# A mixer's output projection by Strassen's seven products instead of eight block products, with its transposes and loads placed anew

## The chip, the cores and the metric

The kernel runs on one core of a Trainium2 chip. The metric is the device time of one execution in microseconds; the time of a kernel is the median over its runs. Engines are called PE (TensorE), DVE (VectorE), ACT (ScalarE), POOL (GpSimd) and SP (SyncE). Each engine works through its own instructions in one fixed order; SP, ACT and POOL also start DMA transfers, each on a queue of its own.

## The reference

One decoder layer on 512 tokens of width 1024, in float32. The part around the change:

```python
y_a = pool_mixer(z_pool, w_pool[i], pool_scale[i]) @ w_branch_a[i]
y_b = spatial_gating(z_uv, sgu_norm[i], w_spatial[i], b_spatial[i]) @ w_branch_b[i]
x = x + (g_a * y_a + g_b * y_b) @ w_out[i]      # the output projection
h = rmsnorm(x, ffn_norm[i])                     # a convolutional FFN and an embedding gate follow
```

`w_out` is 1024 x 1024, as are `w_branch_a` and `w_branch_b`.

## The kernel before

**Numbers in two parts.** Every float32 operand of a matmul is split into a rounded part and a remainder (`hi`, `lo`); `mm3` makes a product of three matmuls (hi·hi, hi·lo, lo·hi). For a weight, `parts` writes `whi` on ACT and `wlo` on DVE; for activations, `split` and `cut_into` do the same (`blk`, `cmb`, `a11`).

**Weights.** A weight arrives in chunks of 512 KB in a buffer `raw`, by SP's queue. `todo` lists all chunks in the order of their use; `prepare` starts up to four loads ahead and `take` keeps up to three chunks split and ready. `whi` and `wlo` have four buffers each, `raw` shares 37 blocks of 4 KB a partition (`blk`) with most activations. The tile framework sets semaphores and decides the order on each engine; a buffer is handed on when its last reader is done.

**Two ways to multiply.** `by_token` does one half of the output columns (`fh`) at a time: four PSUM banks, one for each block of 128 tokens, eight row blocks `k`, 24 matmuls of 512 columns for a chunk. `seven` does a product of 2 x 2 blocks by Strassen's scheme in Winograd's form: seven products `P1` to `P7`, each of half the rows, half the tokens and half the columns, that is 12 matmuls for a chunk of two row blocks (`pairs_of`). `combine` makes the four sums of activation blocks (`D`, `S2`, `S3`, `E`), and `plan_seven` the sums of weight blocks, in one of several ways: with `adds="vector"` DVE adds them, with `"some"` part of them, with `"all"` none: then a DMA of POOL's queue adds a block from memory onto the `raw` buffer (`add_to`). `"P6"`, `"P7"` and `"P4"` accumulate onto two banks `sd` (`seeded`) into which ACT has copied the result of `P1`, and ACT copies them out after `P6` and after `P7` (`copies`).

**The stage in question.** The branch product `yp @ w_branch_a` runs by `by_token` (lines 571 to 576); DVE multiplies it with the gate and adds the other branch into `ga`. `later` is a tiny DVE copy that makes a following DMA wait: the loads of the residual `x` (4 x 512 KB, `xr`) and of the embedding input `pt` (2 x 256 KB, `pT`) go out on ACT's queue. PE transposes `ga` (32 transposes, `turned`), `split` cuts them into `m`, and the output projection runs by `by_token` (lines 622 to 627): 8 chunks, 192 matmuls. Its results are added to `x`. The embedding product (24 matmuls, `embed`), a norm and 32 more transposes follow, then the FFN, whose down projection uses `seven` in the order `DOWN` with `"some"`.

Of the kernel before, what the change touches and what calls it, by code (L numbers as in the profile page):

```python
# [44 lines left out]
def trunk(ctx, tc, xT, xr, pT, wsT, par, bsp, w_u0, w_u1, w_v, w_ga, w_gb, w_p, w_pl,  # L45
# [38 lines left out]
    def pairs_of(n):  # L84

        return [(q, min(2, n - q)) for q in range(0, n, 2)]

    def plan(src, cols=CW, **kw):
        got = []
        todo.append((lambda: got.append(load_raw(src)), lambda: parts(got[0], cols, **kw)))  # L90

    def plan_seven(w, order=INNER, adds="vector", spare=(), q0=0, n=HK):

# [50 lines left out]

        return [unit(prod, ch) for prod in order for ch in pairs_of(n)]

# [33 lines left out]
    for i in range(KD):  # L180
        plan(w_a[i // 4, i % 4].rearrange(flat))
    for i in range(KD):
        plan(w_o[i // 4, i % 4].rearrange(flat))
    for k in range(2):
# [25 lines left out]
    def act(b, sl=slice(None)):  # L210
        return b[:, 0, sl], b[:, 1, sl]
# [30 lines left out]
    def later(t, src):  # L242

        V.tensor_copy(t, src)
# [101 lines left out]

    def seven(op, drain, order=INNER, fill=()):


        fill = list(fill)  # L350
        n = len(op)
        bank_of = {}
# [19 lines left out]

        for prod in order:
            b, c = ops[prod]
            if b not in bank_of:
                bank_of[b] = seeded if b == "b" else [bank() for _ in range(2)]
            o = bank_of[b]
            first = b != "b" and b not in begun
            begun.add(b)
            for ch in pairs_of(n):  # L380
                step(o, c, take(), ch, first)
                if fill:
                    fill.pop(0)()
            if prod == "P1":
                for j in range(2):
                    S.copy(seeded[j], o[j])
            elif prod == "P6":
                copies(0)
            elif prod == "P7":
                copies(1)  # L390
                minus(1)
                for j in range(2):
                    drain(1, j, 1, u[1][j])
            elif prod == "P4":
                for j in range(2):
                    drain(1, j, 0, seeded[j])
            elif prod == "P2":
                for j in range(2):
                    drain(0, j, 0, o[j])
            elif prod == "P3":  # L400
                minus(0)
                for j in range(2):
                    drain(0, j, 1, u[0][j])
# [5 lines left out]

    def by_token(acts, fh, banks, kps, between=None):  # L410

        for kp in kps:
            c = take()
            for b in range(NT):
                for kk in range(2):
                    k = 2 * kp + kk
                    mm3(banks[b], act(acts[k], slice(b * P, (b + 1) * P)), wslice(c, kk, T), k == 0, k == KD - 1)


# [149 lines left out]


    for fh in range(2):
        banks = [bank() for _ in range(NT)] if fh == 0 else [bank(), *seeded, bank()]
        by_token(yp, fh, banks, range(KD // 2))
        for b in range(NT):
            V.tensor_tensor(ga[b][:, fh], banks[b], ga[b][:, fh], op=ALU.mult)
            V.tensor_tensor(ga[b][:, fh], ga[b][:, fh], gb[b][:, fh], op=ALU.add)

    x = [block("x") for _ in range(NT)]
    for b in range(NT):
        later(x[b][:, 0, :1], ga[0][:, 0, :1])  # L580
        nc.scalar.dma_start(x[b].rearrange("p a t -> p (a t)"), xr[b])

    pp = []
    for k in range(2):
        pt = work("pt")
        later(pt[:, :1], ga[0][:, 0, :1])
        nc.scalar.dma_start(pt, pT[k])
        pp.append(act(split(pt)))
# [16 lines left out]

    def columns(z, b, f):

        return z[b][:, f // HK, f % HK * P:(f % HK + 1) * P]

    def turned(z, f):  # L610

        tp = bank()
        for b in range(NT):
            PE.transpose(tp[:, b * P:(b + 1) * P], columns(z, b, f), ident)  # L614
        return tp


    m = []
    for f in range(KD):
        m.append(split(turned(ga, f)))  # L620
    xss = [small.tile([P, 2], F32, tag="xss", name="xss", bufs=NT) for _ in range(NT)]
    for fh in range(2):
        banks = [bank() for _ in range(NT)] if fh == 0 else [*seeded, bank(), bank()]
        by_token(m, fh, banks, range(KD // 2))
        for b in range(NT):
            V.tensor_tensor(x[b][:, fh], banks[b], x[b][:, fh], op=ALU.add)
            squares(b, fh, xss)

# [164 lines left out]
def _layout(i):  # L793
# [9 lines left out]
    def th(w):  # L803
        return w.reshape(KD // 2, 2, P, 2, T).transpose(3, 0, 2, 1, 4)

    def sv(w):
        return w.reshape(2, HK, P, 2, T).transpose(0, 3, 1, 2, 4).reshape(4, HK, P, T)
# [8 lines left out]
    def pairs(z):  # L816
# [21 lines left out]
        "w_b": th(a["w_branch_b"][0]),  # L838
        "w_o": th(a["w_out"][0]),
        "w_up": pairs(up),  # L840

        "w_dn": a["w_down"][0].reshape(KF // 2, 2, P, 2, T).transpose(1, 3, 0, 2, 4).reshape(4, KF // 2, P, T),
        "w_g": a["w_ple_gate"][0].reshape(KD, P, D),
# [18 lines left out]
```

## Time and profile before

| | before |
|---|---|
| median of 3 runs | 785.44 us (785.43 to 786.5) |
| profiled execution: time, span | 785.2 us, 783.5 us |
| PE busy | 770.8 us (98%) |
| DVE busy | 547.7 us (70%) |
| ACT busy | 372.9 us (48%) |
| DMA, mean over the span | 122 GB/s |

The span runs from the first to the last instruction that the profiler saw; what lies outside it is 1.7 us. A busy PE counts overlapping matmuls, so the distance from one matmul's start to the next one's tells more than busy time. In views of time, positions are microseconds from the span's start.

### The profile page before, as it was taken

To read this page: it belongs to the slowest core of one execution; us is meant where nothing else is said; L and a number is where in the kernel's file an instruction comes from. 1 tells how busy PE (TensorE), PEld (TensorE's weight loads), DVE (VectorE), ACT (ScalarE), POOL (GpSimd) and SP (SyncE) were. 2 spreads that over 40 slices of the span, in tenths; PEclk is the share of its full clock that TensorE was granted. 3 is DMA by queue.
4 is the path that set the end of the run, shared out by engine and by line. 5 is a ranking of instruction groups with operands and counts; after the bars stand their busy time and mean duration, and the time that the engine had idled before them with its cause. 6 is when DMAs were issued, how large, how long until landed. Compare 5 with 4: busy or idle time off the path is not lost.

```text
span 783.5 us, 9272 instructions
## 1 busy us (share of the span) xinstructions
PE 770.8 (98%) x3482; PEld 637.6 (81%) x3482; DVE 547.7 (70%) x769; ACT 372.9 (48%) x538; POOL 42.2 (5%) x79
## 2 busy tenths in 40 slices
PE   9999999999999999999999999999999999999896
PEld 7888888888888888888888888888888888877685
DVE  7797798866576734636576778666668767688755
ACT  6576736573232312325545444444445534447723
POOL 0000200000112100001000000000001010000100
PEclk9999999999999999999999999999999999999998
DMA  9712215124132508101832344832336673420411
GB/s 346 276 55 81 80 63 207 54 78 179 40 104 85 215 25 311 67 0 55 324 112 47 108 108 110 274 128 54 82 108 134 209 195 80 122 81 27 135 55 54
DMA packets 36829, 95.35 MB, mean 122 GB/s; under 512 B 3376, under 2 KB 3504, under 8 KB 36784
## 3 DMA queue, kind: packets, MB, share of 16 engines
q1 hardware_dynamic: 32192, 84.68, 30.7%
q0 software_dynamic: 3008, 5.77, 4.7%
q10 hardware_dynamic: 1584, 4.31, 1.7%
q8 instruction: 27, 0.44, 0.2%
q14 instruction: 18, 0.15, 0.1%
HBM read 91.60 MB, written 3.15 MB: 121 GB/s over the span
## 4 chain that ended last, share of the span: by engine, by line
PE 90%; DVE 5%; ACT 2%; DMA 1%; issue 1%; POOL 0%; POOLq 0%; SPq 0%; ACTq 0%; DVEq 0%
PE mm L203 24%; PE mm L204 24%; PE mm L205 24%; PE sd L203 6%; PE sd L204 6%; PE sd L205 6%; DVE wlo L69 2%; ACT whi L68 1%; DMA raw<-in_w_g 1%; DVE raw L137 1%; PE mm L501 1%; PE mm L614 0%; DMA x<-in_xT 0%; DVE xn L649 0%; PE mm L677 0%
## 5 line engine op out<-in xcount | busy, mean ns | idle before, releaser
L69 DVE TENSOR_TENSOR wlo<-raw,whi 128x1024 fp32r<-128x1024 f32 (+1 forms) x186 | 218.0, 1179 | 154.7 <-ACT whi L68 154.0
L68 ACT CAST whi<-raw 128x1024 fp32r<-128x1024 f32 (+1 forms) x179 | 183.7, 1031 | 213.0 <-PE mm L205 59.0
L203 PE MATMUL mm<-blk,whi 128*128 128x512 f32 x480 | 187.1, 392 | 0.1
L204 PE MATMUL mm<-blk,whi 128*128 128x512 f32 x480 | 186.8, 389 | 0.0
L205 PE MATMUL mm<-blk,wlo 128*128 128x512 f32 x480 | 186.6, 389 | 0.0
L203 PEld LDWEIGHTS mm<-blk,whi 128*128 128x128 f32 x480 | 90.5, 189 | 19.3 <-ACT blk L238 0.4
L204 PEld LDWEIGHTS mm<-blk,whi 128*128 128x128 f32 x480 | 90.2, 188 | 18.8
L205 PEld LDWEIGHTS mm<-blk,wlo 128*128 128x128 f32 x480 | 90.1, 188 | 18.7
L203 PE MATMUL mm<-whi,blk 128*128 128x512 f32 x210 | 82.1, 391 | 0.0
L204 PE MATMUL mm<-wlo,blk 128*128 128x512 f32 x210 | 81.8, 390 | 0.0
L205 PE MATMUL mm<-whi,blk 128*128 128x512 f32 x210 | 81.7, 389 | 0.0
L205 PEld LDWEIGHTS mm<-whi,blk 128*128 128x128 f32 x210 | 39.4, 188 | 8.2
L203 PEld LDWEIGHTS mm<-whi,blk 128*128 128x128 f32 x210 | 39.4, 188 | 8.2 <-DVE blk L236 0.2
L204 PEld LDWEIGHTS mm<-wlo,blk 128*128 128x128 f32 x210 | 39.4, 188 | 8.1
L203 PE MATMUL sd<-whi,blk 128*128 128x512 f32 x114 | 44.8, 393 | 0.3 <-ACT u L367 0.3
L204 PE MATMUL sd<-wlo,blk 128*128 128x512 f32 x114 | 44.4, 389 | 0.0
L205 PE MATMUL sd<-whi,blk 128*128 128x512 f32 x114 | 44.4, 389 | 0.0
L137 DVE TENSOR_TENSOR raw<-raw 128x1024 f32<-128x1024 f32 (+1 forms) x36 | 42.0, 1198 | 0.1
L203 PE MATMUL sd<-whi,cmb 128*128 128x512 f32 x92 | 36.2, 395 | 0.8 <-ACT u L367 0.8
L204 PE MATMUL sd<-wlo,cmb 128*128 128x512 f32 x92 | 36.1, 392 | 0.8 <-DVE wlo L69 0.8
L203 PE MATMUL mm<-whi,cmb 128*128 128x512 f32 x92 | 35.9, 390 | 0.0
L205 PE MATMUL sd<-whi,cmb 128*128 128x512 f32 x92 | 35.8, 390 | 0.0
(168 smaller groups left out, 1048.5 us busy)
## 6 DMA issues: line engine op xcount, KB each, us to landing
raw<-in_w_up SPq DMA_DIRECT2D x44, 512.0 KB, 4.9
raw<-in_w_dn SPq DMA_DIRECT2D x25, 512.0 KB, 3.7
raw<-in_w_dn POOLq DMA_DIRECT2D x10, 512.0 KB, 5.9
raw<-in_w_v SPq DMA_DIRECT2D x8, 512.0 KB, 11.1
raw<-in_w_ga SPq DMA_DIRECT2D x8, 512.0 KB, 3.9
raw<-in_w_gb SPq DMA_DIRECT2D x8, 512.0 KB, 3.6
raw<-in_w_p SPq DMA_DIRECT2D x8, 512.0 KB, 4.9
raw<-in_w_b SPq DMA_DIRECT2D x8, 512.0 KB, 3.9
```

Source lines behind the costliest of these rows:

```text
L68: (V.tensor_copy if first else S.copy)(hi[:, :cols], raw[:, :cols])
L69: V.tensor_tensor(lo[:, :cols], raw[:, :cols], hi[:, :cols].bitcast(F32), op=ALU.subtract)
L137: V.tensor_tensor(z[:, :cols], z[:, :cols], raw[extra, ch][:, :cols], op=ALU.add)
L203: PE.matmul(o, wh, ah, start=first, stop=False, **kw)
L204: PE.matmul(o, wh, al, start=False, stop=False, **kw)
L205: PE.matmul(o, wl, ah, start=False, stop=last, **kw)
L501: PE.matmul(mx[:, n * P:(n + 1) * P], vt[n].rearrange("p a t -> p (a t)")[:, f * P:(f + 1) * P], wsm[:, f, :], start=True, stop=True)
```

## The change

The projection `w_out` now goes through `seven` in the order `DOWN`, with the weights' sums made by DMA alone (`"all"`), and with `crossed=True`, which swaps the second and third of the 14 steps: P1's first chunk, P5's first, P1's second, P5's second, then the others in order. The transposes and `combine` of a pair of row blocks are a function, `turn_pair`. Pairs 0 and 1, which need only the first half of `ga`, are turned inside the second half of the branch product; pairs 2 and 3 as `fill`, behind the first and the second step of the projection. The loads of `x` and `pt` wait for the second half of `ga` instead of the first.

```diff
+    def steps_of(order, n, crossed=False):
+        steps = [(prod, ch) for prod in order for ch in pairs_of(n)]
+        if crossed:
+            steps[1], steps[2] = steps[2], steps[1]
+        return steps
...
-        return [unit(prod, ch) for prod in order for ch in pairs_of(n)]
+        return [unit(prod, ch) for prod, ch in steps_of(order, n, crossed)]
...
-    for i in range(KD):
-        plan(w_o[i // 4, i % 4].rearrange(flat))
+    todo.extend(plan_seven(blocks(w_o), DOWN, "all", crossed=True))
...
-    def seven(op, drain, order=INNER, fill=()):
+    def seven(op, drain, order=INNER, fill=(), n=None, crossed=False):
...
-        n = len(op)
+        n = n or len(op)
...
-        for prod in order:
+        for prod, ch in steps_of(order, n, crossed):
...
-            begun.add(b)
-            for ch in pairs_of(n):
-                step(o, c, take(), ch, first)
-                if fill:
-                    fill.pop(0)()
+            if ch[0] + ch[1] == n:
+                begun.add(b)
+            step(o, c, take(), ch, first)
+            if fill:
+                fill.pop(0)()
+            if ch[0] + ch[1] < n:
+                continue
...
-    def by_token(acts, fh, banks, kps, between=None):
+    def by_token(acts, fh, banks, kps, after=()):
+        after = list(after)
...
+            if after:
+                after.pop(0)()
...
+    def turn_pair(q):
+        s = []
+        for f in (2 * q, 2 * q + 1):
+            tp = turned(ga, f)
+            s.append(work("s"))
+            S.copy(s[-1], tp)
+        s1, s2 = s
+        if q % 2 == 0:
+            m11.append(block("a11", (2, 2, H), F32R))
+        t = m11[-1][:, q % 2]
+        cut_into(t, s1[:, :H])
+        z = combine(s1, s2)
+        a2 = split(s2)
+        m.append(dict(A11=t, A12=a2[:, :, :H], A22=a2[:, :, H:], **z))
...
-        by_token(yp, fh, banks, range(KD // 2))
+        early = [nothing, lambda: turn_pair(0), lambda: turn_pair(1)] if fh else ()
+        by_token(yp, fh, banks, range(KD // 2), early)
...
-        later(x[b][:, 0, :1], ga[0][:, 0, :1])
+        later(x[b][:, 0, :1], ga[b][:, 1, :1])
...
-        later(pt[:, :1], ga[0][:, 0, :1])
+        later(pt[:, :1], ga[NT - 1][:, 1, :1])
...
-    for f in range(KD):
-        m.append(split(turned(ga, f)))
...
-    for fh in range(2):
-        banks = [bank() for _ in range(NT)] if fh == 0 else [*seeded, bank(), bank()]
-        by_token(m, fh, banks, range(KD // 2))
-        for b in range(NT):
-            V.tensor_tensor(x[b][:, fh], banks[b], x[b][:, fh], op=ALU.add)
-            squares(b, fh, xss)
+    def drain_m(th, j, fh, src):
+        b = 2 * th + j
+        V.tensor_tensor(x[b][:, fh], src, x[b][:, fh], op=ALU.add)
+        squares(b, fh, xss)
+    seven(m, drain_m, DOWN, [lambda: turn_pair(2), lambda: turn_pair(3)], HK, crossed=True)
```

The rest lays `w_out` out by blocks, as `w_down` already was.

**What the order on the engines is.** Lines are those of the kernel that a fence shows; words in brackets are the semaphores that an instruction waits on. First ACT, around the loads of `x` and `pt`. Before (`whi` are chunks of `w_a` and `w_out`):

```order
L581 DMA x_2521<-in_xr 128x1024 [waits DVE_49]
L581 DMA x_2522<-in_xr 128x1024 [waits DVE_49]
L581 DMA x_2523<-in_xr 128x1024 [waits DVE_49]
L68 CAST whi_2455<-raw_2353 128x1024 [waits DMAHW2_49,PE_49,Activation_49]
L581 DMA x_2524<-in_xr 128x1024 [waits DVE_49]
L587 DMA pt_2533<-in_pT 128x512 [waits DMAHW3_49,DVE_49,Pool_49]
L587 DMA pt_2539<-in_pT 128x512 [waits DMAHW4_49,DVE_49]
L235 CAST blk_2536<-pt_2533 128x512 [waits DMAHW3_49]
L68 CAST whi_2485<-raw_2393 128x1024 [waits PE_49,Activation_49]
L235 CAST blk_2542<-pt_2539 128x512 [waits DMAHW4_49]
L68 CAST whi_2622<-raw_2423 128x1024 [waits PE_49,Activation_49]
L68 CAST whi_2652<-raw_2453 128x1024 [waits DMAHW5_49,PE_49,Activation_49]
```

After, at the projection's start (`whi_2720` is P2's first chunk, `s` are pair 2's transposes on their way out of PSUM, `a11_2652` is pair 2's part of A11, which P1's second chunk multiplies):

```order
L68 CAST whi_2720<-raw_2548 128x1024 [waits DMAHW6_49,PE_49]
L622 DMA x_2587<-in_xr 128x1024 [waits DVE_49]
L622 DMA x_2588<-in_xr 128x1024 [waits DVE_49]
L622 DMA x_2589<-in_xr 128x1024 [waits DVE_49]
L622 DMA x_2590<-in_xr 128x1024 [waits DVE_49]
L628 DMA pt_2599<-in_pT 128x512 [waits DMAHW3_49,DVE_49]
L628 DMA pt_2605<-in_pT 128x512 [waits DVE_49]
L601 COPY s_2643<-mm_2638 128x512 [waits PE_49]
L601 COPY s_2650<-mm_2645 128x512 [waits PE_49]
L241 CAST blk_2602<-pt_2599 128x512 [waits DMAHW3_49]
L241 CAST blk_2608<-pt_2605 128x512 [waits DMAHW4_49]
L336 CAST a11_2652<-s_2643 128x256 [waits Activation_49]
```

The loads now stand behind the casts of the projection's own weights, and the two casts of `pt`, each waiting for its load, stand between pair 2's copies and the cast of pair 2's A11.

Second POOL, whose queue had no transfer of `w_out` before. After, its eight additions from memory (`raw_2393` and `raw_2486` are the buffers that hold in turn the weights of P5, P6 and P4, first and second chunk; `raw_2738` and `raw_2757` are those of P7):

```order
L112 DMA raw_2393<-in_w_o 128x2x512 [waits DMAHW3_49,PE_49]
L112 DMA raw_2393<-in_w_o 128x2x512 [waits DMASW0_49,DVE_49]
L112 DMA raw_2486<-in_w_o 128x2x512 [waits DMAHW5_49,PE_49]
L112 DMA raw_2486<-in_w_o 128x2x512 [waits DMASW2_49,DVE_49]
L112 DMA raw_2393<-in_w_o 128x2x512 [waits DMASW1_49,DVE_49]
L112 DMA raw_2738<-in_w_o 128x2x512 [waits DMAHW7_49,DMAHW6_49,PE_49]
L112 DMA raw_2757<-in_w_o 128x2x512 [waits DMAHW1_49,DMAHW7_49,DMAHW0_49,PE_49]
L112 DMA raw_2486<-in_w_o 128x2x512 [waits DMASW3_49,DVE_49]
```

The first and third make P5's weights, the second and fourth P6's, the fifth and eighth P4's, the sixth and seventh P7's. The second, fourth, fifth and eighth wait for DVE, which must have read the buffer's former contents: the fifth for P6's first chunk.

Third ACT, at the projection's sixth and seventh product (`whi_2760`, `whi_2777` are P6's chunks, `whi_2800`, `whi_2818` P7's, `u` the copies of P6's result out of the banks `sd`, on which P7 goes on):

```order
L68 CAST whi_2760<-raw_2393 128x1024 [waits DMASW1_49]
L68 CAST whi_2777<-raw_2486 128x1024 [waits DMASW3_49,PE_49]
L645 ACTIVATE sq_2795,xss_2614<-x_2587 128x512 [waits DMAHW7_49,DVE_49]
L645 ACTIVATE sq_2798,xss_2615<-x_2588 128x512 [waits DMAHW0_49,DVE_49]
L68 CAST whi_2800<-raw_2738 128x1024 [waits DMASW5_49,PE_49]
L68 CAST whi_2818<-raw_2757 128x1024 [waits DMASW6_49,PE_49]
L373 COPY u_2834<-sd_129 128x512 [waits PE_49]
L373 COPY u_2836<-sd_130 128x512 [waits PE_49]
```

No such rows stood before: there the projection had a cast for each chunk and nothing to copy. The casts of P7's weights, each waiting for an addition of POOL's queue, stand ahead of the copies that P7's matmuls wait for.

## Rows read from the trace of the kernel before

**Rows 1.** The profile page: busy time of each engine; granted clock by slice

```profile
PE 770.8 (98%) x3482; PEld 637.6 (81%) x3482; DVE 547.7 (70%) x769; ACT 372.9 (48%) x538; POOL 42.2 (5%) x79
...
PEclk9999999999999999999999999999999999999998
```

**Rows 2.** Longest waits of PE: total us, times, longest us

```profile
PE mm L204 <- DVE wlo L69: 2.0, 2, 1.7
```

**Rows 3.** Timeline of PE around the transposes of ga: start us, us, instruction

```profile
315.68 0.39 PE L205 MATMUL mm<-whi,blk 128*128 128x512 f32 x1
315.91 2.48 PE L614 MATMUL mm<-ident,sg 128*128 128x128 f32 x20
318.66 1.85 PE L614 MATMUL mm<-ident,sg 128*128 128x128 f32 x12 [0.27 <-DVE blk L236]
320.45 0.50 PE L203 MATMUL mm<-whi,blk 128*128 128x512 f32 x1
```

**Rows 4.** Timeline of PE at the projection's end

```profile
363.88 0.39 PE L205 MATMUL mm<-whi,blk 128*128 128x512 f32 x1
364.11 0.39 PE L203 MATMUL mm<-whi,blk 128*128 128x512 f32 x1
...
369.55 4.56 PE L614 MATMUL mm<-ident,xn 128*128 128x128 f32 x32
```

**Rows 5.** Windows: busy PE, PEld, DVE, ACT, POOL; clock, DMA share, GB/s

```profile
325.00:360.00 35.00, 35.00 (x156) 28.99 (x155) 10.15 (x13) 9.96 (x15) 0.00 (x0) 1.00 0.00 1
```

**Rows 6.** Timeline of ACT and its DMA queue (ACTq) in the branch product

```profile
294.35 3.36 ACTq L581 DMA_DIRECT2D x<-in_xr  x3
...
299.86 0.34 ACTq L581 DMA_DIRECT2D x<-in_xr  x1
300.31 1.02 ACTq L587 DMA_DIRECT2D pt<-in_pT  x2
308.42 0.62 ACT L235 CAST blk<-pt 128x512 fp32r<-128x512 f32 x1 [7.53 <-DMA pt<-in_pT]
...
309.90 0.61 ACT L235 CAST blk<-pt 128x512 fp32r<-128x512 f32 x1
```

**Rows 7.** Busy time and DMA while x and pt load (columns as in Rows 5)

```profile
296.00:308.00 12.00, 12.00 (x55) 9.93 (x54) 2.75 (x7) 1.05 (x1) 0.00 (x0) 1.00 1.00 381
```

**Rows 8.** The profile page: DMA queues, and the issues of w_dn on POOL

```profile
q1 hardware_dynamic: 32192, 84.68, 30.7%
q0 software_dynamic: 3008, 5.77, 4.7%
...
raw<-in_w_dn POOLq DMA_DIRECT2D x10, 512.0 KB, 5.9
```

**Rows 9.** Groups of DVE instructions by shape: busy us, mean ns, idle before

```profile
L69 DVE TENSOR_TENSOR wlo<-raw,whi 128x1024 fp32r<-128x1024 f32 x171 | 208.0, 1222 | 147.7 <-ACT whi L68 147.1
```

**Rows 10.** Groups of ACT instructions by shape (columns as in Rows 9)

```profile
L68 ACT CAST whi<-raw 128x1024 fp32r<-128x1024 f32 x171 | 179.1, 1051 | 211.2 <-PE mm L205 59.0 <-PE mm L204 56.3 <-issue 37.6
...
L367 ACT COPY u<-sd 128x512 f32<-128x512 f32 x24 | 13.8, 588 | 8.3 <-PE sd L205 8.1
```

**Rows 11.** Windows at the kernel's end (columns as in Rows 5)

```profile
776.00:778.00 2.00, 0.38 (x4) 0.17 (x2) 1.03 (x3) 0.63 (x2) 0.00 (x0) 1.00 0.00 0
778.00:780.00 2.00, 0.00 (x0) 0.00 (x0) 0.89 (x3) 1.04 (x3) 0.55 (x1) 0.68 0.00 0
780.00:783.50 3.50, 0.00 (x0) 0.00 (x0) 0.00 (x0) 0.00 (x0) 0.00 (x0) 0.50 0.40 152
```

**Rows 12.** Timeline of PE at the kernel's start

```profile
5.43 2.05 PE L203 MATMUL mm<-blk,whi 128*128 128x512 f32 x4
7.30 0.41 PE L204 MATMUL mm<-blk,whi 128*128 128x512 f32 x1
```

**Rows 13.** Timeline of DVE behind the projection

```profile
368.59 1.67 DVE L649 TENSOR_SCALAR xn<-x,fr 128x512 f32<-128x512 f32 x4 [0.53 <-POOL fr L599]
```

More of the change, by code (lines that the diff above doesn't have):

```diff
@@ L90, in plan, with plan_seven @@
         todo.append((lambda: got.append(load_raw(src)), lambda: parts(got[0], cols, **kw)))
-    def plan_seven(w, order=INNER, adds="vector", spare=(), q0=0, n=HK):
+    def plan_seven(w, order=INNER, adds="vector", spare=(), q0=0, n=HK, crossed=False):
         raw = {}
@@ L568, in trunk, with columns, turned @@
             group_maps(i // 5)
+    def columns(z, b, f):
+        return z[b][:, f // HK, f % HK * P:(f % HK + 1) * P]
+    def turned(z, f):
+        tp = bank()
+        for b in range(NT):
+            PE.transpose(tp[:, b * P:(b + 1) * P], columns(z, b, f), ident)
+        return tp
+    m = []
+    m11 = []
+    def turn_pair(q):
[12 more added lines that the diff above has]
+        m.append(dict(A11=t, A12=a2[:, :, :H], A22=a2[:, :, H:], **z))
     for fh in range(2):
         banks = [bank() for _ in range(NT)] if fh == 0 else [bank(), *seeded, bank()]
-        by_token(yp, fh, banks, range(KD // 2))
+        early = [nothing, lambda: turn_pair(0), lambda: turn_pair(1)] if fh else ()
+        by_token(yp, fh, banks, range(KD // 2), early)
         for b in range(NT):
@@ L604, in squares @@
         S.activation(sq, x[b][:, fh], AF.Square, accum_out=sums[b][:, fh:fh + 1])
[L606 to L612, printed above, removed]
-        for b in range(NT):
-            PE.transpose(tp[:, b * P:(b + 1) * P], columns(z, b, f), ident)
-        return tp
-    m = []
-    for f in range(KD):
-        m.append(split(turned(ga, f)))
-    xss = [small.tile([P, 2], F32, tag="xss", name="xss", bufs=NT) for _ in range(NT)]
-    for fh in range(2):
-        banks = [bank() for _ in range(NT)] if fh == 0 else [*seeded, bank(), bank()]
-        by_token(m, fh, banks, range(KD // 2))
-        for b in range(NT):
-            V.tensor_tensor(x[b][:, fh], banks[b], x[b][:, fh], op=ALU.add)
-            squares(b, fh, xss)
+    xss = [small.tile([P, 2], F32, tag="xss", name="xss", bufs=NT) for _ in range(NT)]
+    def drain_m(th, j, fh, src):
[3 more added lines that the diff above has]
+    seven(m, drain_m, DOWN, [lambda: turn_pair(2), lambda: turn_pair(3)], HK, crossed=True)
     c_ple = [take(), take()]
@@ L804, in th, with alt @@
         return w.reshape(KD // 2, 2, P, 2, T).transpose(3, 0, 2, 1, 4)
+    def alt(w):
+        n = w.shape[0] // P // 2
+        return w.reshape(n, 2, P, 2, T).transpose(1, 3, 0, 2, 4).reshape(4, n, P, T)
     def sv(w):
@@ L838, in _layout @@
         "w_b": th(a["w_branch_b"][0]),
-        "w_o": th(a["w_out"][0]),
+        "w_o": alt(a["w_out"][0]),
         "w_up": pairs(up),
-        "w_dn": a["w_down"][0].reshape(KF // 2, 2, P, 2, T).transpose(1, 3, 0, 2, 4).reshape(4, KF // 2, P, T),
+        "w_dn": alt(a["w_down"][0]),
         "w_g": a["w_ple_gate"][0].reshape(KD, P, D),
```

## The prediction

> **What bounds the kernel now.** I read the page first: PE is busy for 98% of the span at full granted clock [rows 1]. The view of PE's waits then shows how little it waits: the largest entry is 2.0 us in two waits, far from this stage [rows 2]. So a matmul saved is time saved, and a new wait of PE is time lost. The timeline gives the price of a matmul: the projection's first one starts at 320.45, the first one behind it at 364.11 [rows 3, 4]; 43.7 us for 192 are 0.227 us each (the 0.39 us of a row overlap). Last I looked at what stands ready to be loaded with work: in the projection's middle DVE is busy for 10.2 of 35 us, ACT for 10.0, and DMA moves 1 GB/s [rows 5]. All three get much more to do, so the question is not how much but in which order.
>
> **What is saved.** Eight chunks of 24 matmuls become 14 of 12, 168 for 192: 24 x 0.227 = 5.5 us less. The 32 transposes stay; 20 of them take 2.48 us [rows 3], 0.12 us each, wherever they stand.
>
> **First wait: ACT stands behind the loads of pt.** The order of ACT shows the place: four loads of x, two of pt, pair 2's two copies, the two casts of pt, and only then the cast of pair 2's A11, which P1's second chunk needs. Before, only weight casts stood behind the casts of pt: ACT waited 7.53 us there, ending at 308.42 [rows 6], and PE, with three chunks ready, felt nothing. The positions after, in the clock of the old trace:
>
> 315.91 was the end of the branch product's issue [rows 3]. Pairs 0 and 1 now come ahead of it: 16 x 0.12 = 1.9 us, so P1's first chunk runs from 317.8 to 320.5 (12 x 0.227), six of the next transposes to 321.2, then P5's first chunk.
>
> The cast ahead of the loads needs the buffer of P1's first weights, free at 320.9, and takes 1.05 us [rows 10]. The loads of x go out from 322.0. Six issues of 0.34 to 0.5 us [rows 6] and DVE's last sum of ga bring pair 2's copies to 324.7 to 325.8. One of the banks of P5's second half is freed by such a copy: PE, there at 322.7, goes on at 325.4. That is 2.7 us. P5's chunk and four transposes then end at 327.3.
>
> Before, the second cast of pt began 15.5 us after the first issue of x (294.35 to 309.90) [rows 6], with DMA full at 381 GB/s [rows 7]: 4.6 MB in 12 us, of which x and pt are 2.6 MB and four weight chunks nearly all the rest. After, x is issued in some 2 us instead of 5.5, but weight chunks for the projection still come beside it, and one adding transfer. I take the same 15.5 us: second cast at 337.5, then 0.6 and 0.4 us for it and A11, and P1's second chunk starts at 338.5. PE waits 11.2 us.
>
> Together 13.9 us. Bounds: x and pt alone need 6.9 us at 381 GB/s, and about 2.6 us are fixed (5.9 us to landing less 3.3 of transfer, next part): 9.5 us instead of 15.5, together 7.9. With the adding transfer on top of the old mixture (3.3 us), 17.2. The old mixture is the nearest row.
>
> **Behind it.** The second half of the crossed chunks needs pair 3's copy out of PSUM, five subtractions and casts, with ACT working off its backlog (seven instructions of about 0.55 us until the last A11). PE has 12 matmuls and some transposes meanwhile. I count 2 us of small waits, from 0 to 4.
>
> **Second wait: POOL's queue is in order.** With weights summed by DMA alone there are eight adding transfers. Their price: the software queue moved 5.77 MB in 4.7% of the span's 783.5 us, 157 GB/s, the hardware queue 84.68 MB in 30.7%, 352 GB/s [rows 8]. So 0.52 MB take 3.3 us, and 5.9 us from issue to landing [rows 8]. In POOL's order the addition for P4 stands ahead of both for P7, and it waits until DVE has read P6's first chunk. Counted from the restart R = 338.5:
>
> ACT's twelve instructions up to P6's cast are 7 us of work; two of them wait for P1's last matmuls, so the cast ends at about R + 9.5. DVE's part takes 1.2 us [rows 9]: R + 10.7.
>
> Then the additions follow one another: P4's lands at R + 16.6, P7's at R + 19.9 and R + 23.2. The cast of the latter (1.05 us [rows 10]) stands ahead of ACT's copies of P6's result (0.59 us [rows 10]); P7 may not write those banks before: P7 starts at R + 25.1.
>
> PE needs for P1, P5, P2 and P6 72 matmuls, 16.4 us, with 0.5 us of transposes and the 2 us of waits: R + 18.9.
>
> PE waits 6.2 us. Bounds: none, if an addition moves as fast as a load (0.52 MB at 352 GB/s, 1.5 us: P7's weights at R + 18), and 10 if weight loads run beside it. I take 6.2, since all the additions in the rows give the 3.3 us.
> The Trainium skill ("DMA: Bandwidth & Descriptors", section "Anatomy of one DMA — SWDGE (gpsimd) path") prices a transfer of this queue at 2.0 us plus bytes over 436 GB/s, an estimate of 3.2 us here. Rows 8 have 5.9 us; by the page's price the second wait would be gone and the sum 6.2 us lower.
>
> **The end.** The last xn is made from 368.59 to 370.26 [rows 13]; 24 embedding matmuls (5.4 us) cover the way there, and the 32 transposes after them take 4.56 instead of 3.8 us [rows 4]. With P3 last, DVE has two subtractions more of 0.6 us ahead of this, and its queue is fuller: 1.5 us, from 0 to 3.
>
> **The clock.** After PE's last matmuls, 0.4 us into 776 to 778, the granted clock is 0.68 in 778 to 780 and 0.50, the lower level of 1.2 GHz, from 780 [rows 11]. An idle time of 11 us should do the same. At the kernel's start four matmuls take 1.87 us, 0.47 each [rows 12], twice 0.227 and some waits. I take 10 to 20 matmuls at the lower level, 2 to 4 us, of which the second wait swallows part: 2.5 us, from 0 to 5.
>
> **Sum.** -5.5 + 13.9 + 2.0 + 6.2 + 1.5 + 2.5 = +20.6 us. The profiled execution took 785.2 us, 0.2 below the median of the runs: 805.8, and 806 against that median.
>
> **The rivals.**
>
> The additions are quick, or the first wait has let them run ahead: no second wait, -5.5 + 13.9 + 2 + 1.5 + 2 = +13.9, 799 us. For it: DMA is idle late in the stage. Against: P4's addition can't be issued before P6's chunk is split, and the two behind it can't pass it.
>
> pt lands early: x is issued at once and nothing delays it, first wait 7.9: 800 us. Against: in the trace pt took the bandwidth of others' 2 MB with it.
>
> Everything collides: the first wait 17.2, the second 10, the clock 4: 785.2 + 20.6 + 3.3 + 3.8 + 1.5 = 814 us.
>
> The other side: the gain stands. ACT gets past pt before PE needs A11; the saving remains, less the end: -5.5 + 1.5, 781 us. This needs pt cast by 327.3, 5.3 us after the first load of x goes out, and P7's weights by R + 18. Rows 6 have 15.5 us for the first.
>
> Nothing changes by more than 1.6 us (0.2%, about what a measurement of this kernel tells from no change): only if waits happen to equal the saving.
>
> **How the numbers follow.** Both waits as forecast: 0.62, with a range of its own of 800 to 812. Quick additions 0.15, early pt 0.10, collision 0.08, gain 0.04, no change 0.01. The range 798 to 812 leaves out the last three, 0.13. Slower in all but the last two: 0.95.
>
> **What would show it.** In the profile after: PE starts 24 matmuls fewer; ACT's waits name pt with about 11 us ahead of its cast; PE's longest wait is for ACT's A11 at P1's second chunk, preceded by one of 2 to 3 us in P5's first; ACT's casts of P7 wait for DMA, and PE waits for `u` or those casts; the granted clock dips behind the first. I would be wrong if pt's casts come without a wait, or if PE reaches P7 before DMA has become quiet and yet doesn't wait.

## The result, and the profile after

| | before | after |
|---|---|---|
| median | 785.58 us (785.43 to 786.5, 4 runs) | 802.89 us (801.95 to 803.85, 4 runs) |
| profiled execution: span | 783.5 us | 800.7 us |

The change makes the kernel slower: ratio 1.0224, with a 95% interval of 1.0212 to 1.0236.

The page of the kernel after answers to [rows 1]. PE's share falls from 98% to 96%, and the 17th of the 40 slices of the granted clock (320 to 340 us) falls from 9 tenths or more to 6.

```profile
PE 770.2 (96%) x3458; PEld 634.9 (79%) x3458; DVE 566.4 (71%) x803; ACT 390.2 (49%) x566; POOL 51.6 (6%) x87
...
PEclk9999999999999999699999999999999999999999
```

The longest waits of PE in the kernel after, as in [rows 2] (total us, times, longest us):

```profile
PE mm L209 <- ACT a L336: 7.8, 1, 7.8
PE sd L209 <- ACT u L373: 5.5, 3, 4.4
PE mm L210 <- DVE wlo L69: 2.3, 3, 1.7
PE mm L209 <- ACT s L601: 2.2, 1, 2.2
...
PE mm L590 <- DVE xn L677: 1.1, 1, 1.1
```

The first, the fourth and the last are new, and so is the longest of the second (4.4 us; the other two, 1.1 us together, were there before). The third was there before with 2.0 us. The first is P1's second chunk, which waits for pair 2's A11; the second holds P7, which waits for the banks that the copies `u` free; the fourth is in P5's first chunk, which waits for a bank that a copy `s` frees; the last are the transposes of xn. Below I count a wait as the distance from one matmul's start to the next one's less the usual 0.227 us. That comes to some 0.2 to 0.3 us more than the idle time that this view shows: 8.1, 4.6 and 2.3 us, and 1.3 for xn.

ACT and its queue in the kernel after (start us, us, instruction, and in brackets the idle time before it):

```profile
321.12 2.26 ACTq L622 DMA_DIRECT2D x<-in_xr  x4
323.47 0.97 ACTq L628 DMA_DIRECT2D pt<-in_pT  x2
324.48 1.08 ACT L601 COPY s<-mm 128x512 f32<-128x512 f32 x2 [3.34 <-DVE wlo L69]
332.35 0.62 ACT L241 CAST blk<-pt 128x512 fp32r<-128x512 f32 x1 [6.79 <-DMA pt<-in_pT]
334.73 0.62 ACT L241 CAST blk<-pt 128x512 fp32r<-128x512 f32 x1 [1.76 <-DMA pt<-in_pT]
335.25 0.40 ACT L336 CAST a<-s 128x256 fp32r<-128x256 f32 x1
...
355.82 1.04 ACT L68 CAST whi<-raw 128x1024 fp32r<-128x1024 f32 x1 [4.24 <-DMA raw<-in_w_o]
358.39 1.04 ACT L68 CAST whi<-raw 128x1024 fp32r<-128x1024 f32 x1 [1.53 <-DMA raw<-in_w_o]
359.35 1.07 ACT L373 COPY u<-sd 128x512 f32<-128x512 f32 x2
```

Here both waits can be read in their order. The cast of A11 (335.25) is free of any wait of its own; it starts when ACT is through with the second pt, and PE starts at 335.70. The copies `u` (359.35) stand behind the cast of P7's second chunk, which waits for a DMA, and PE starts P7 at 359.98. From the first issue of x to the second cast of pt it is 13.6 us, where [rows 6] had 15.5.

POOL's queue in the kernel after:

```profile
323.25 1.20 POOL L112 DMA_DIRECT2D raw<-in_w_o  x1 [13.52 <-DVE pt L250]
347.51 4.87 POOL L112 DMA_DIRECT2D raw<-in_w_o  x4 [23.06 <-DVE wlo L69]
```

The queue stands for 23 us until DVE has split P6's first chunk, and then issues four additions in a row, P4's and P7's. The windows of the same kernel (columns as in [rows 5]):

```profile
300.00:310.00 10.00, 10.00 (x50) 8.37 (x49) 5.43 (x10) 4.40 (x8) 2.42 (x2) 1.00 0.10 7
...
320.00:326.00 6.00, 3.67 (x19) 2.42 (x18) 4.67 (x13) 2.12 (x3) 1.20 (x1) 1.00 0.64 225
326.00:328.00 2.00, 1.88 (x8) 1.18 (x6) 0.35 (x2) 0.00 (x0) 0.00 (x0) 0.59 0.99 325
...
326.00:335.70 9.70, 1.88 (x8) 1.18 (x6) 1.70 (x5) 1.59 (x4) 0.00 (x0) 0.52 1.03 311
335.70:340.00 4.30, 4.30 (x12) 3.44 (x13) 3.56 (x7) 3.09 (x6) 0.00 (x0) 0.50 1.04 422
...
355.40:360.00 4.60, 0.15 (x2) 0.03 (x1) 1.75 (x2) 2.65 (x4) 0.00 (x0) 1.00 1.08 192
360.00:364.00 4.00, 4.00 (x11) 3.13 (x12) 3.05 (x3) 2.30 (x3) 0.00 (x0) 0.57 0.15 26
```

The clock is at its lower level (0.50, 1.2 GHz) in the longer part of the first wait and behind it, up to 340 us, and behind the second (0.57 as the mean of 360 to 364). It falls the first time between 326 and 328 us: PE has just begun again after the 2.3 us at P5, and the 8.1 us at P1 are still to come. DMA is at a full share in both waits, but in the second it moves only 192 GB/s: what runs there are the additions. And ten us in which DMA could have loaded ahead are empty (7 GB/s at 300 to 310). The waits of SP's queue from 290 to 340 us tell more of that:

```profile
SPq L112 <- PE mm L211: 24.6, 1, 24.6
SPq L112 <- DMA x<-in_xr: 16.9, 3, 13.7
```

Three loads of the projection's weights could not be issued for 16.9 us because they waited for loads of x. In the kernel before, loads on SP waited so for 7.0 us. The trace tells why: SP's loads and ACT's report their landing on the same eight completion counters, and a load on SP waits until the counter that it will use itself is free. The four loads of x and the two of pt land at 324.44, 325.70, 328.42, 329.62, 332.33 and 334.70 us; the next six loads on SP, each on the counter of one of these, go out at 324.50, 325.75, 328.48, 329.69, 332.39 and 334.77.

### The profile page after: what moved, and what is told of

It is laid out like the page before. It is cut to its first block, busy times and chain, and to the rows that moved or that the text cites. A ratio compares the mean times of both kernels' runs of the same rounds, so it can differ in the third digit from the quotient of the medians.

```text
span 800.7 us, 9323 instructions
## 1 busy us (share of the span) xinstructions
PE 770.2 (96%) x3458; PEld 634.9 (79%) x3458; DVE 566.4 (71%) x803; ACT 390.2 (49%) x566; POOL 51.6 (6%) x87
## 4 chain that ended last, share of the span: by engine, by line
PE 79%; issue 9%; DMA 4%; DVE 4%; ACT 2%; POOL 1%; POOLq 0%; SPq 0%; ACTq 0%; DVEq 0%
PE mm L209 20%; PE mm L211 20%; PE mm L210 20%; PE sd L209 6%; PE sd L210 6%; PE sd L211 6%; DMA raw<-in_w_o 3%; DVE wlo L69 1%; DMA raw<-in_w_g 1%; ACT whi L68 1%; PE mm L512 1%; DVE raw L144 1%; DMA x<-in_xT 0%; DVE u L377 0%; DVE xn L677 0%
## 5 line engine op out<-in xcount | busy, mean ns | idle before, releaser
L69 DVE TENSOR_TENSOR wlo<-raw,whi 128x1024 fp32r<-128x1024 f32 (+1 forms) x192 | 224.9, 1179 | 147.6 <-ACT whi L68 147.0
L68 ACT CAST whi<-raw 128x1024 fp32r<-128x1024 f32 (+1 forms) x185 | 189.8, 1032 | 203.1 <-PE mm L210 56.7
L209 PE MATMUL mm<-whi,blk 128*128 128x512 f32 x170 | 66.7, 392 | 0.4 <-ACT sd L394 0.4
L210 PE MATMUL mm<-wlo,blk 128*128 128x512 f32 x170 | 66.3, 390 | 0.0
L211 PE MATMUL mm<-whi,blk 128*128 128x512 f32 x170 | 66.2, 389 | 0.0
L209 PE MATMUL sd<-whi,cmb 128*128 128x512 f32 x108 | 43.1, 401 | 5.2 <-ACT u L373 5.2
L209 PE MATMUL mm<-whi,cmb 128*128 128x512 f32 x108 | 42.6, 394 | 2.3 <-ACT s L601 2.2
L210 PE MATMUL sd<-wlo,cmb 128*128 128x512 f32 x108 | 42.9, 397 | 0.8 <-DVE wlo L69 0.8
L211 PE MATMUL sd<-whi,cmb 128*128 128x512 f32 x108 | 42.8, 396 | 0.0
L210 PE MATMUL mm<-wlo,cmb 128*128 128x512 f32 x108 | 42.5, 393 | 0.0
L211 PE MATMUL mm<-whi,cmb 128*128 128x512 f32 x108 | 42.3, 392 | 0.0
L209 PE MATMUL sd<-whi,blk 128*128 128x512 f32 x106 | 41.6, 393 | 0.3 <-ACT u L373 0.3
L211 PE MATMUL sd<-whi,blk 128*128 128x512 f32 x106 | 41.3, 389 | 0.0
L209 PEld LDWEIGHTS mm<-whi,blk 128*128 128x128 f32 x170 | 31.9, 188 | 7.3 <-ACT sd L394 0.9
```

What stands on the lines that cost most here:

```text
L68: (V.tensor_copy if first else S.copy)(hi[:, :cols], raw[:, :cols])
L69: V.tensor_tensor(lo[:, :cols], raw[:, :cols], hi[:, :cols].bitcast(F32), op=ALU.subtract)
L209: PE.matmul(o, wh, ah, start=first, stop=False, **kw)
L210: PE.matmul(o, wh, al, start=False, stop=False, **kw)
L211: PE.matmul(o, wl, ah, start=False, stop=last, **kw)
```

## The experiments

Two questions were put. First: is it ACT's and POOL's order, as forecast, or the later condition on the loads itself, that costs the time? Second: are the two waits independent, or is there a limit behind both, namely what DMA has to move? All times are to be read beside 802.9 us for the kernel after and 785.1 to 785.6 for the one before, which ran again beside each of them; the kernel after did not. The expectations quote 8.1, 4.6 and 2.3 us for the three waits.

**The early condition restored.**

```diff
-        later(x[b][:, 0, :1], ga[b][:, 1, :1])
+        later(x[b][:, 0, :1], ga[0][:, 0, :1])
...
-        later(pt[:, :1], ga[NT - 1][:, 1, :1])
+        later(pt[:, :1], ga[0][:, 0, :1])
```

> The kernel after, but with the early condition on the loads of x and pt that the kernel before had (both wait for the first half of ga's first block only, instead of the last sums). If the late condition is what brings pt late, the loads go out some microseconds before the branch product's end, the first wait (2.3 + 8.1 us in the profile after) shrinks by up to the 4 to 6 us that x's loads are earlier, and the time is 797 to 799 us. If the loads are late for another reason (their place behind the early pairs' copies, and the blocks that they are put into come free late), the condition decides nothing: 802 to 804 us and the first x issue again about 5 us behind the end of the branch product's matmuls.

Measured: 803.73 us (802.96 to 804.11). The first x goes out at 321.60 us, directly behind the weight cast at 320.57 as in the kernel after. The later condition decides nothing there: the loads already stand late in ACT's order.

**The late condition alone, in the kernel before.**

```diff
-        later(x[b][:, 0, :1], ga[0][:, 0, :1])
+        later(x[b][:, 0, :1], ga[b][:, 1, :1])
...
-        later(pt[:, :1], ga[0][:, 0, :1])
+        later(pt[:, :1], ga[NT - 1][:, 1, :1])
```

> The kernel before, with only the late condition on the loads of x and pt taken from the change (no seven products, no early transposes). ACT's pt casts stand ahead of the casts of the transposed activations there too, so if the loads are moved from 294 to about 321 us, some 21 us of cover are lost: the second pt cast is at about 316 + 3 + 13.6 = 333 us instead of 310, and PE, which has all transposes but few split activations, waits at the projection's start: 785.6 + 10 to 14 = 796 to 800 us. If the loads' time is not the cause of the first wait, the time stays at 785.6 us.

Measured: 798.67 us (797.9 to 798.8), ratio 1.0163 (1.0142 to 1.0184). ACT in this kernel:

```profile
315.29 3.56 ACTq L581 DMA_DIRECT2D x<-in_xr  x4
318.94 0.88 ACTq L587 DMA_DIRECT2D pt<-in_pT  x2
326.42 0.62 ACT L235 CAST blk<-pt 128x512 fp32r<-128x512 f32 x1 [10.08 <-DMA pt<-in_pT]
328.31 0.62 ACT L235 CAST blk<-pt 128x512 fp32r<-128x512 f32 x1 [1.27 <-DMA pt<-in_pT]
```

PE waits 11.9 us, here inside the transposes of ga, and the clock is low behind it. So late loads of x and pt cost 13 us without any of the seven products: a wait of the first kind needs nothing of Strassen's scheme, only ACT's order and late loads.

**pt's casts behind the projection.**

```diff
-        pp.append(act(split(pt)))
+        pts.append(pt)
...
     seven(m, drain_m, DOWN, [lambda: turn_pair(2), lambda: turn_pair(3)], HK, crossed=True)
+    for pt in pts:
+        pp.append(act(split(pt)))
```

> The kernel after, with the casts of the two pt tiles moved in the program from ahead of the projection to behind it; the loads stay. The theory that ACT, in order, holds A11's cast behind two casts that wait for pt: the 8.1 us wait at P1's second chunk goes, with the low clock behind it (some 1.9 us); if the weights' chain then moves forward with it, 803 - 10 = 793 us. The rival that the transfers themselves (x, pt and eight additions) limit the stage: the wait moves to P7, whose additions can't land much earlier, the 4.6 us there become 11 to 13, and the time is 797 to 800 us. If pt's casts don't hold anything, 803 us.

Measured: 800.71 us (800.37 to 801.47). The wait at P1's second chunk is gone, as the first theory has it, but the time falls by 2.2 us only: the wait at P7 is 11.9 us instead of 4.6, and one of 1.6 us is new, at pair 3's transposes, which wait for a bank (a copy `s`). ACT there, in the kernel with pt's casts late:

```profile
351.75 1.04 ACT L68 CAST whi<-raw 128x1024 fp32r<-128x1024 f32 x1 [9.89 <-DMA raw<-in_w_o]
355.03 1.99 ACT L68 CAST whi<-raw 128x1024 fp32r<-128x1024 f32 x2 [2.24 <-DMA raw<-in_w_o]
```

POOL issues the four additions at 336.74 now, 10.8 us sooner than in the kernel after, yet P7's first chunk is cast only 4.1 us sooner: P7's two additions take 14.2 and 16.8 us from issue to landing. This is the rival's result, 0.7 us above its range.

**Fewer additions by DMA.**

```diff
-    todo.extend(plan_seven(blocks(w_o), DOWN, "all", crossed=True))
+    todo.extend(plan_seven(blocks(w_o), DOWN, "some", crossed=True))
```

(The expectation names two of the products wrongly: DVE makes P6's and P4's sums in this mode, DMA those of P5 and P7. P4's is gone from POOL's queue all the same.)

> The kernel after, with the weights of the projection summed in the mode that leaves the additions for P5 and P4 to VectorE, so that only P6's and P7's chunks are summed by adding transfers, four instead of eight. The theory of two separate waits: P4's addition no longer stands ahead of P7's, the 4.6 us at P7 and the low clock behind it (1.6 us) go, the first wait stays at some 10 us, so 796 to 797 us. If adding transfers also take bandwidth from x and pt, or hold PE's first weights, the first wait shrinks as well by one or two transfers of 3.3 us: 790 to 794 us. If the additions don't matter, 803 us, and if VectorE's extra sums (8 of 1.0 to 1.2 us) come onto the path, more.

Measured: 794.97 us (793.46 to 795.38). P7's wait is 0.6 us, and P1's has shrunk to 4.9: four additions less helped pt, too, by 3 us. The time is 1 us above the forecast for this (790 to 794).

**P4's additions behind P7's.**

```diff
-                if adds == "all" and prod in ("P5", "P6"):
-                    add_to(z, "c" if prod == "P5" else "d", ch)
+                if adds == "all" and prod == "P5":
+                    add_to(z, "c", ch)
+                if adds == "all" and prod == "P6":
+                    with tc.issue_after(sums[-1].ins):
+                        add_to(z, "d", ch)
```

(`sums` lists the additions for P7's chunks.)

> The kernel after, with the two additions for P4 issued behind both additions for P7 in POOL's queue; nothing else moved. The theory that P4's addition, waiting for P6's first chunk, holds up P7's: the 4.6 us at P7 and the low clock behind them (some 1.6 us) go, the first wait stays: 802.9 - 6.2 = 797 us. The rival that the transfers are late by themselves: P7's additions come only one transfer of 3.3 us sooner, 1.3 us and part of the low clock stay: 799 to 800 us. If the order in that queue decides nothing, 803 us.

Measured: 798.74 us (797.14 to 801.8). POOL's queue in this kernel:

```profile
323.98 2.42 POOL L113 DMA_DIRECT2D raw<-in_w_o  x2 [13.54 <-DVE pt L256]
336.34 1.20 POOL L113 DMA_DIRECT2D raw<-in_w_o  x1 [9.95 <-DMA raw<-in_w_o]
348.48 2.42 POOL L113 DMA_DIRECT2D raw<-in_w_o  x2 [10.94 <-DVE wlo L69]
```

P7's additions no longer wait for P6, the wait at P7 is 0.2 us instead of 4.6, and P1's is 8.6. The median lies between the two forecasts and the four runs spread over 4.7 us; the trace decides. With the first wait in place, the order of POOL's queue is the whole of the second.

**Both repairs together.** The edits of the run with pt's casts late and of the one just shown.

> Both single repairs at once: pt's casts behind the projection (alone it gave 2.2 us, and the wait at P7 grew from 4.6 to 11.9 us) and P4's additions behind P7's. If the order of POOL's queue is what made that wait grow, it goes now: 800.7 - 11.9 - 2 for the low clock = 787 us. The rival that P7's weights are late by the amount of transfers ahead of them (x, pt, w_o's loads and the additions for P5, P6 one after the other): P7's last addition lands at about the same time after the stage's start as in that run, less at most one transfer of 3.3 us: 797 to 800 us.

Measured: 796.1 us (795.83 to 797.11). A wait of 7.5 us stays at P7, so that without the first wait the order of POOL's queue is worth 4.4 of the 11.9 us. The rest is not only P7's late weights. ACT in this kernel:

```profile
346.55 1.04 ACT L68 CAST whi<-raw 128x1024 fp32r<-128x1024 f32 x1 [4.41 <-DMA raw<-in_w_o]
351.62 1.04 ACT L68 CAST whi<-raw 128x1024 fp32r<-128x1024 f32 x1 [4.03 <-DMA raw<-in_w_o]
352.57 1.06 ACT L379 COPY u<-sd 128x512 f32<-128x512 f32 x2
```

The first row is the cast of P7's second chunk, the last of P7's weights (its addition lands at 346.47). The second is the cast of P4's first chunk, which waits for P4's addition (351.52) and here stands ahead of the copies `u`. With `u` directly behind P7's cast, P7 could start at about 348.1 instead of 353.2 (an estimate from these rows): some 5 of the 7.5 us are once more ACT's order, and 2.5 the landing of P7's addition. That addition went out at 336.19, as soon as the load that it adds onto had landed (335.63); SP had held this load for x until 324.55. With pt's casts late alone, P4's cast stands ahead of `u` too, but its addition has landed before. No run puts `u` ahead of these casts.

**Half of the additions and pt's casts late.** The edits of those two runs.

> Half of the additions taken from DMA (VectorE adds P6's and P4's chunks) and pt's casts behind the projection. The first alone left a wait of 4.9 us at P1's second chunk with some 13 slow matmuls and 0.6 us at P7 (795.0 us). If ACT's two casts were all that was left there, 795 - 4.9 - 2 = 788 us, and no new wait. If the transfers still limit P7, 2 to 4 us come back there: 790 to 792 us. Against the kernel before, the saving of 5.5 us would then stand against some 2.3 us at P5's second half, 2.5 at the xn transposes and 2 to 4 of low clock and small waits.

Measured: 791.16 us (790.43 to 792.33), the upper of the two forecasts: 2.4 us have come back at P7, where ACT's second copy `u` (349.82 us) again stands behind a cast that waits for an addition (348.87).

**No addition by DMA, pt's casts late.** The mode is `"vector"`, eight plain loads.

> The kernel after, with all sums of the weights made by VectorE (eight plain loads of 0.5 MB, no adding transfer, eight additions of 1.0 to 1.2 us on VectorE) and pt's casts behind the projection. If DMA's work for the sums is what is left of the second wait (2.4 us at P7 in the run with half of them), it goes: 791.2 - 2.4 - 0.5 = 788 us, with the 2.3 us at P5's second half and the xn waits left. If VectorE, which then has 80 to 90% to do in the stage's middle, becomes late with wlo or the sums, PE waits there instead: 790 to 794 us.

Measured: 786.49 us (785.71 to 787.28), ratio to before 1.0015 (1.0006 to 1.0024). This is below both forecasts. P7 no longer waits, and DVE, at 93% from 320 to 355 us, holds PE up only at the end (1.0 and 1.5 us at the transposes of xn); the 2.3 us at P5 are still there. The same window in the kernel with all additions and pt's casts late, and then in this one:

```profile
320.00:355.00 35.00, 22.16 (x101) 16.75 (x99) 18.16 (x35) 13.63 (x23) 6.07 (x5) 0.94 1.00 297
```

```profile
320.00:355.00 35.00, 32.75 (x142) 25.83 (x141) 32.59 (x49) 23.28 (x37) 0.00 (x0) 0.95 0.50 196
```

DMA is busy for all of the 35 us in the one and for half in the other. In the first there is no room left in this window. That does not make DMA the limit of the whole stage: ahead of the window, in the same kernel, it is far from full, while loads on SP wait 20.9 us for loads of x.

```profile
300.00:310.00 10.00, 10.00 (x50) 8.37 (x49) 5.44 (x10) 4.38 (x8) 2.42 (x2) 1.00 0.23 61
310.00:320.00 10.00, 10.00 (x51) 8.32 (x50) 8.54 (x17) 5.15 (x8) 0.00 (x0) 1.00 0.55 98
```

**Also x and pt loaded by POOL's queue.** The edits of half of the additions and late casts, and:

```diff
-        nc.scalar.dma_start(x[b].rearrange("p a t -> p (a t)"), xr[b])
+        nc.gpsimd.dma_start(x[b].rearrange("p a t -> p (a t)"), xr[b])
...
-        nc.scalar.dma_start(pt, pT[k])
+        nc.gpsimd.dma_start(pt, pT[k])
```

> The same as the run with half of the additions on VectorE and pt's casts late, and the six loads of x and pt issued from POOL's queue instead of ACT's. If the 2.3 us at P5's second half are ACT's issues (2.3 + 0.9 us) standing ahead of pair 2's copies, they go, and the additions for P7 keep their time: 3 to 5 us below that run, 781 to 785 us, faster than the kernel before by 0 to 0.6%. If these loads now hold up the additions behind them in POOL's queue, or the low software queue brings x late for the first drain, the gain is lost at P7 and the time is 786 to 790 us.

Measured: 783.91 us (783.2 to 785.03), ratio to before 0.9984 (0.9975 to 0.9993). The 2.3 us at P5 and the wait at P7 are gone. ACT's issues were thus most of the 2.3 us: the copies of pair 2 come at 323.62 and wait for PE's transposes alone. What took P7's wait away can be followed from SP's queue. Without the move (first row) it waits, from 290 to 340 us, for x; with it no row names x, and the longest is the second:

```profile
SPq L112 <- DMA x<-in_xr: 26.3, 2, 25.5
```

```profile
SPq L112 <- PE mm L211: 28.6, 3, 23.1
```

In the stretch from 310 to 320 us DMA moves 182 GB/s with the move and nothing without. So the loads that P7's additions add onto are there sooner, and POOL issues these additions at 326.42 us instead of 333.82, though x and pt now stand ahead of them in its queue. The two effects of this edit weren't run apart.

**The order of xn.** In the loop that makes xn, `for b in range(NT)` becomes `for b in (2, 3, 0, 1)`; once on top of the version just shown, once in the kernel after alone.

> The fastest version so far (half of the additions on VectorE, pt's casts late, x and pt loaded by POOL's queue: 783.9 us) with one line more: xn is made for the token blocks in the order 2, 3, 0, 1, the order in which the seven products finish them, instead of 0, 1, 2, 3. In that run the rows of blocks 2 and 3 were ready some 6 us before those of 0 and 1, but stood behind them on VectorE, and PE waited 1.27 us for the last xn and 1.15 us behind it. The theory that the end's cost is this order: the 1.27 us go, 782.6 us, and at most the 1.15 us as well, 781.5. The rival of the forecast, that P3's two additional subtractions make the end late: nothing changes, 783.9 us.

> The kernel after, with only that line: xn in the order 2, 3, 0, 1. If the end stands by itself, the 1.26 us for xn go, 802.9 - 1.3 = 801.6 us, and the two waits before are as they were (8.1 and 4.6 us). If it isn't the order that makes xn late, 802.9 us.

Measured: 782.54 us (782.16 to 784.46), ratio to before 0.9969 (0.9958 to 0.998); and 802.13 us (800.81 to 807.1), too wide to tell from 802.9 by itself. DVE in the kernel after:

```profile
382.20 1.67 DVE L677 TENSOR_SCALAR xn<-x,fr 128x512 f32<-128x512 f32 x4 [0.63 <-POOL fr L640]
...
384.78 1.68 DVE L677 TENSOR_SCALAR xn<-x,fr 128x512 f32<-128x512 f32 x4 [0.58 <-POOL fr L640]
```

and in the kernel after with the other order:

```profile
376.38 1.28 DVE L677 TENSOR_SCALAR xn<-x,fr 128x512 f32<-128x512 f32 x3 [0.60 <-POOL fr L640]
...
383.70 1.67 DVE L677 TENSOR_SCALAR xn<-x,fr 128x512 f32<-128x512 f32 x4 [0.55 <-POOL fr L640]
```

Three of the four pieces for blocks 2 and 3, which the seven products finish first, are made 8 us sooner (in the kernel after they are the group at 384.78), and the last group is through 1.1 us sooner. PE's two waits there, 1.26 and 1.15 us, become 0.49 and 0.68 in both kernels. In the first kernel's profile, which is of the slowest of its seven runs (784.46 us), a wait of 1.8 us at P7 is back: x's loads and the additions land later there (x 7.4 to 12.7 us after issue, 5.3 to 7.2 in the version before). The rest of the end is DVE's chain behind P3.

**The wait filled with work of no use.** The four transposes ahead of P1's second chunk are made 18 times.

```diff
-        for b in range(NT):
+        for b in [*range(NT)] * (18 if z is ga and f == 6 else 1):
             PE.transpose(tp[:, b * P:(b + 1) * P], columns(z, b, f), ident)
```

> The kernel after with additional work of no use: the four transposes that stand ahead of P1's second chunk are made 18 times instead of once (68 more, at 0.11 to 0.12 us some 7.5 to 8.4 us, in the 8.1 us in which PE waits). The theory that the idle time lowers the clock: the granted clock is full in P1's second chunk and behind it, its matmuls are 0.227 us apart instead of 0.427, some 2 us less up to there; 801 us if nothing behind takes it back, 803 if pair 3's copies or P7's weights do. The rival that the low clock has another cause (DMA at its full rate, for instance): the clock stays at one half from 326 to 340 us, the transposes last twice as long, and the time is 803 to 811 us.

Measured: 805.41 us (803.97 to 806.14). The windows of this kernel (columns as in [rows 5]):

```profile
328.00:330.00 2.00, 2.00 (x21) 2.00 (x19) 0.00 (x0) 0.00 (x0) 0.00 (x0) 1.00 0.98 314
...
336.00:338.00 2.00, 0.57 (x2) 0.30 (x2) 0.90 (x2) 1.45 (x3) 0.00 (x0) 1.00 1.05 414
338.00:340.00 2.00, 0.90 (x3) 0.30 (x2) 1.91 (x5) 1.50 (x3) 0.00 (x0) 0.78 1.02 418
340.00:342.00 2.00, 0.88 (x5) 0.88 (x5) 1.83 (x3) 1.48 (x3) 0.00 (x0) 0.50 1.04 426
```

While PE transposes, the clock is full, with DMA at its full share: DMA is not what lowers it. It falls at 339, behind the 2.2 us of wait that are left and at the start of a new one of 2.4 us, in which PE waits for a bank of pair 3 (a copy `s` that now comes late). So the clock falls after idle time of PE and not with DMA's load; in the kernel after it is low from 362 to 364 us, too, with DMA idle. The time, in the range of the rival, decides nothing: it doesn't isolate the clock's price, since the filler brought the wait for that bank.

## Why the prediction held, and where its sizes were off

The forecast was 806 us, 798 to 812; 802.9 came, by the mechanism forecast. The table holds the terms against the trace of after.

| term | forecast, us | measured, us | from |
|---|---|---|---|
| 24 matmuls | -5.5 | -5.5 | 168 for 192, 0.227 apart where nothing waits |
| first wait | +13.9 | +10.5 | 2.3 at P5 and 8.1 at P1's second chunk |
| behind it | +2.0 | +0.9 | 0.6 at P2, and 0.3 at P5's first matmul, ahead of the first wait |
| second wait | +6.2 | +4.6 | P7 |
| end | +1.5 | +2.1 | 2.9 at the transposes of xn, 0.8 before |
| clock | +2.5 | +3.3 | two times 8 starts some 0.2 us later than usual, most of them at 336 to 339 and at 361 to 364 |
| sum | +20.6 | +15.9 | the spans differ by 800.7 - 783.5 = 17.2 |

The measured terms leave 1.3 us. Some 0.6 of it are six transposes at the lower clock, 0.21 us apart instead of 0.12; the rest is spread over distances too small to list and over the other stages.

**First wait.** Place and cause hold: without pt's casts ahead of A11 the 8.1 us are gone. The mis-sized term is this one: its 3.4 us are as much as the whole difference between 20.6 and 17.2. That the other misses (-1.1, -1.6, +0.6 and +0.8 us) and the 1.3 us left over cancel is luck. Two of the steps were long: the loads of x start at 321.1 and not at 322.0, and pt takes 13.6 us from there, not 15.5. I had noted that x is issued faster than before and still taken the old 15.5 us as the nearest row; the lower bound had 9.5. That an early pt would not suffice to save the kernel was right: with nothing waiting for pt the time was 800.7 us.

**Behind it.** The 0.9 us are within the 0 to 4, but not what I had described: 0.6 are a wait of P2 for ACT's copy of P1's result (`sd`), for which ACT itself had waited for PE, and 0.3 come ahead of the first wait. ACT's backlog of casts cost nothing that the trace shows.

**Second wait.** The chain was foreseen link by link. From P1's restart R (335.70 us), P4's addition was forecast to go out at R + 10.7 and went out at R + 11.8; the casts of P7 were forecast at R + 19.9 and R + 23.2 and came at R + 20.1 and R + 22.7; P7 at R + 25.1 (the forecast's own terms, 23.2 + 1.05 + 0.59, give 24.8), came at R + 24.3. PE was there at R + 19.7 and not R + 18.9, since the low clock, which I had counted apart, falls into this stretch. The order of POOL's queue is shown as its cause by the run that turns it. The price of an addition was 3.3 us; the two casts are 2.57 apart. By the estimate of 3.2 us to landing from the Trainium skill ("DMA: Bandwidth & Descriptors", section "Anatomy of one DMA — SWDGE (gpsimd) path") there would have been no such wait; the page of the profile has 8.4 us to landing as the median of the eight, and the measurement decides.

```profile
q0 software_dynamic: 5184, 9.96, 7.6%
...
raw<-in_w_o POOLq DMA_DIRECT2D x8, 512.0 KB, 8.4
```

Against [rows 8], the eight additions brought the software queue 4.2 MB.

**What the sum hid.** I added the waits as if each could be had back alone. They can't: the repair of the first gave 2.2 us, because the second grew by 7.3 and 1.6 us came up at pair 3. Behind the growth are three things that the runs show but don't weigh against each other: DMA, busy for 35 of 35 us with pt's casts late; SP's loads, which wait for x while DMA has time; and ACT's copies `u`, which stand behind the casts of P7 and, there, of P4. The rival "the additions are quick" had an idle DMA late in the stage for it; the run with pt's casts late shows that this idle time is there only as long as the first wait makes everybody late. POOL's chain follows P1's restart there as well (the additions go out 9.9 us behind P1's second chunk), but an addition then takes up to 16.8 us to land.

**What I had not seen.** Weight loads on SP wait for loads of x (16.9 us of waits, 7.0 before). I counted what stands behind ACT's instructions and POOL's and didn't look at the waits of SP's queue, which showed it already in the trace of before. ACT's order so holds up a third queue: SP stands from 310.7 to 324.4 us for a load of x that ACT issues at 321.1. It is part of why DMA is empty at 300 to 310 us and full from 326 to 340. How much of the 17 us is due to it alone stays open: in the version with x and pt on POOL's queue it is gone together with ACT's issues.

**The end.** Right in sum, half wrong in cause: the order in which xn was made, and not the two subtractions, cost 1.2 of the 2.1 us. The other 0.9 lie in DVE's chain behind P3, of which the two subtractions are part; they weren't run apart.

**The clock.** Right in cause (it is full while the wait is filled) and within its range; the forecast had 10 to 20 slow matmuls with part of them swallowed, there were 16. It fell sooner than forecast, behind the 2.3 us at P5 and not in the long wait.

**The gain.** It exists: with half of the additions on DVE, pt's casts behind the projection, x and pt on POOL's queue and xn in the order of the products, the seven products run in 782.5 us, 0.31% (0.2 to 0.42) below the kernel before, about half of the 5.5 us that 24 matmuls are worth. As its profile has a wait of 1.8 us at P7, the second wait is not safely gone in this version. The kernel before wasn't run with x and pt on POOL's queue; little could come of it, as its PE waits 0.3 us in all from 300 to 380 us.

## What to carry to other kernels

An instruction that waits for a transfer holds all that stands behind it on its engine, and a DMA issue that waits holds its queue: before a load is made later, list what follows its first reader and what shares its queue and its completion counters. If a trace shows two waits in one stage, repair them together, look at the share of DMA over the whole stage before adding up their gains, and read the order on the engine anew after each repair: here another cast came to stand ahead of the copies. Sums of weights made by DMA keep DVE free only as long as DMA has the time: here eight of them used what the loads needed.

## What the runs showed of the hardware that I had not expected

- An addition by DMA uses the engines longer than a load: in the second wait, with nothing but the software queue's transfers under way, the share was full (1.08) at 192 GB/s; from 335.7 to 340 us, with nothing but plain loads, it was 1.04 at 422 GB/s.
- Loads on SP's queue wait for loads that ACT's queue issued: 16.9 us in the kernel after, 26.3 in the one with half of the additions and pt late, none when these loads went through POOL's queue. The reason is in the trace: the program has eight completion counters for the transfers of SP and ACT together and eight others for POOL's, and six loads in a row on SP went out 0.05 to 0.07 us after the load with the same counter had landed.
- The clock can fall when PE already works again: behind the 2.3 us at P5 it was full until 326 us and low from there on in the kernel after, and in the run with half of the additions on DVE the matmuls from 325.8 to 327.1 us are 0.427 apart. Behind the same wait it stayed full in the run with pt's casts late alone (1.00 from 325 to 330 us) and in the one with the filled wait (1.00 from 326 to 328); what decides between the two no run shows.
